# Add and tanh-GELU over 1024 x 4096: other block widths, and a first store that waits for a load

## The chip, the core and the metric

The kernel runs on one core of a Trainium2 chip. The time is device microseconds of one execution; lower is better. The engines that matter here are VectorE (DVE in the profile), ScalarE (ACT), GpSimd (POOL) and SyncE (SP), which issues every DMA of this kernel. The transfers themselves are carried by the core's 16 DMA engines.

## The reference

Two fp32 arrays are added, and the tanh form of GELU is taken of the sum:

```python
def reference(x, y):          # both 1024 x 4096, float32
    z = x + y
    return 0.5 * z * (1 + np.tanh(np.sqrt(2 / np.pi) * (z + 0.044715 * z ** 3)))
```

Each input and the output have 16.78 MB (16384 KB), so 33.55 MB are read and 16.78 MB are written, whatever the tiling.

## The kernel before, in words

The operation is elementwise, so the kernel may cut the arrays as it likes. It sees each array as 128 partitions with `TOT` = 32768 elements in each, and cuts this into three blocks (`blocks`, line 88). A block is one contiguous piece of the DRAM array, laid out as 128 rows, one row for each partition. The rows have 61.25 KB (15680 elements), 64 KB (16384) and 2.75 KB (704). The narrow block comes first in the numbering of columns (0 to 704) and last in DRAM; `rows` (line 90) finds the place. One DMA moves one block of one array, so there are nine transfers: three of x, three of y, three of the output. Each has 128 packets, one for each row.

All of x stays in SBUF in the tile `zt` (named z in the profile); sums and results overwrite it in place. y's narrow block has a tile of its own, `ys`; y's two wide blocks share one tile `yt` (y in the profile) of half the width. So y's second wide block can only be loaded when all adds of the first half that read `yt` are done (`needs[load_y]`, line 188).

SP issues the nine transfers in a fixed order (lines 180 and 181):

```python
sp = [(load_y, 0), (load_y, 1), (load_x, 1), (load_x, 2), (load_y, 2), (load_x, 0)]
sp += [(store, i) for i in (1, 0, 2)]
```

Number 0 is the narrow block, 1 the first wide block, 2 the second. So the order is: y narrow, y first wide, x first wide, x second wide, y second wide (after the adds), x narrow, and then the stores: first wide, narrow, second wide. `begin_early` (line 9) moves the first two of them ahead of the program's opening, and `wait_late` (line 23) moves the wait for the last transfer to the end of the program. Neither is changed.

The compute works on 20 chunks of up to 2048 columns (`chunks`, line 103), numbered by column: chunk 0 is the narrow block, 1 to 8 the first wide block, 9 to 19 the second. A chunk is added by VectorE or GpSimd (`on_vector`, `on_gpsimd`, line 161), and then ScalarE takes the GELU in place (line 173). For some chunks (`copies`, line 104) ScalarE first copies x into PSUM (line 155), and VectorE's add reads it there. GpSimd's first add in the first half is held until VectorE's add of chunk 1 is done (`held`), since it is to run beside adds that read one operand from PSUM. Each engine works through its list in the written order (`on_vector`, `on_gpsimd`, `on_scalar`), under a manual schedule; a store waits for the GELUs of its block (`needs[store]`, line 195).

Of the kernel before, what the change touches and what calls it, by code (L numbers as in the profile page):

```python
# [66 lines left out]
def kernel(  # L67
# [12 lines left out]
    nc = tc.nc  # L80
# [4 lines left out]
    N, D = x.shape  # L85
    assert N % P == 0
    TOT = N // P * D
    blocks = [(704, 16384), (16384, TOT), (0, 704)]

    def rows(array, lo, hi):  # L90
        flat, at = array.rearrange("n d -> (n d)"), 0
        for f, e in blocks:
            if f <= lo and hi <= e:
                own = flat[P * at : P * (at + e - f)].rearrange("(p c) -> p c", p=P)
                return own[:, lo - f : hi - f]
            at += e - f
        raise AssertionError((lo, hi))

    HALF, SLIM = TOT // 2, 704
    xloads = [SLIM, 15680, HALF]  # L100
    yloads = [SLIM, 15680, HALF]
    stores = [SLIM, 15680, HALF]
    chunks = [704, 1344] + [2048] * 7 + [512, 1536] + [2048] * 6 + [1024, 512, 512]
    copies = {2: 0, 3: 2048, 4: 0, 5: 2048, 6: 0, 9: 0, 10: 512, 11: 2048}
    on_vector = [1, 2, 3, 4, 5, 6, 9, 10, 11, 0, 13, 14, 15, 16, 17, 18, 19]
    on_gpsimd = [7, 8, 12]
    on_scalar = [("copy", c) for c in (2, 3, 4, 5, 6)] + [("gelu", 1)] + [("copy", c) for c in (9, 10, 11)] + [("gelu", c) for c in [*range(2, 13), 0, *range(13, 20)]]
    held = {7: 1}

    def ranges(sizes):  # L110
        ends = [sum(sizes[: i + 1]) for i in range(len(sizes))]
# [16 lines left out]
    zt = pool_sb.tile([P, TOT], fp32, tag="z", name="z")  # L128
    yt = pool_y.tile([P, HALF], fp32, tag="y", name="y")
    ys = pool_y.tile([P, SLIM], fp32, tag="ys", name="ys")  # L130
    ps = pool_ps.tile([P, 4096], fp32, tag="ps", name="ps")
    adds = {}

    def in_psum(c):
        a, b = cr[c]
# [6 lines left out]
    def in_y(a, b):  # L142
        return ys[:, a:b] if b <= SLIM else yt[:, a % HALF : a % HALF + b - a]

    def load_y(i):
        a, b = yr[i]
        nc.sync.dma_start(out=in_y(a, b), in_=rows(y, a, b))  # L147

    def store(i):
        a, b = sr[i]  # L150
        nc.sync.dma_start(out=rows(out, a, b), in_=zt[:, a:b])

    def copy(c):
        a, b = cr[c]
# [20 lines left out]
    def earlier_user(c):  # L175
        lo, hi = copies[c], copies[c] + chunks[c]
        before = [k for k in copies if k < c and copies[k] < hi and copies[k] + chunks[k] > lo]
        return [(add, k) for k in before]

    sp = [(load_y, 0), (load_y, 1), (load_x, 1), (load_x, 2), (load_y, 2), (load_x, 0)]  # L180
    sp += [(store, i) for i in (1, 0, 2)]
    pool = [(add, c) for c in on_gpsimd]
    dve = [(add, c) for c in on_vector]
# [5 lines left out]
        copy: lambda c: [(load_x, i) for i in over(xr, *cr[c])] + earlier_user(c),  # L189
        add: lambda c: [(load_x, i) for i in over(xr, *cr[c])]  # L190
        + [(load_y, i) for i in over(yr, *cr[c])]
        + [(copy, k) for k in copies if k == c]
        + [(add, k) for h, k in held.items() if h == c],
# [55 lines left out]
```

## Time and profile before

| | us |
|---|---|
| median of 3 runs | 122.71 (122.63 to 122.83) |
| the profiled execution, its time | 120.94 |
| the profiled execution, its span | 119.5 |
| DVE / ACT / POOL busy in it | 29.2 / 44.1 / 13.8 |

The profiled execution is one run; its span goes from its first to its last instruction or landing, and its time is 1.4 us longer than that. Its rows therefore add up to the span, not to the median of the runs.

In the profile L140 is a load of x, L147 a load of y, L151 a store, L155 a copy to PSUM, L161 an add and L173 a GELU. An engine's name with a q (SPq) is its sequencer: an SPq row is the issue of a DMA, and the DMA lands later. In the view of stretches, DMA packets are counted in the stretch in which they start, with their whole size and time, so the figures of short stretches jump.

### The profile page before, as it was taken

The page shows a single profiled execution, that of the slowest core. Times are in us where ns is not written, and L with a number is a line of the kernel's source. Part 1 is how long each engine was busy: PE and PEld are TensorE (multiplying, and loading weights), DVE is VectorE, ACT ScalarE, POOL GpSimd, SP SyncE. Part 2 cuts the span into 40 slices and gives each one's busy share as a digit, 9 for nine tenths or more (in the row PEclk, how much of TensorE's full clock was granted, in tenths as well). Part 3 has the DMA queues.
Part 4 walks back from the last instruction along what each step waited for, and adds up shares of the span by engine and source line. Part 5 has one row for each costly group of instructions (what it writes and reads, how often), then busy time and mean ns, then how long its engine had stood idle before and what let it go on. Part 6 is the DMA issues. An engine that isn't in the chain of part 4 may idle for free.

```text
span 119.5 us, 118 instructions
## 1 busy us (share of the span) xinstructions
DVE 29.2 (24%) x18; ACT 44.1 (37%) x30; POOL 13.8 (12%) x7
## 2 busy tenths in 40 slices
DVE  0000000000000599970000000029999920000000
ACT  4000000000000588830099999406799980000000
POOL 0000000000000099900000000029200000000000
DMA  9779879977987898889888988997998789998991
GB/s 457 336 336 651 357 336 441 567 336 336 651 357 336 351 702 351 351 351 680 373 351 351 680 373 351 351 457 336 399 567 378 336 362 534 571 395 351 417 571 66
DMA packets 1296, 50.33 MB, mean 421 GB/s; under 512 B 144, under 2 KB 144, under 8 KB 528
## 3 DMA queue, kind: packets, MB, share of 16 engines
q1 hardware_dynamic: 1296, 50.33, 98.6%
HBM read 33.55 MB, written 16.78 MB: 421 GB/s over the span
## 4 chain that ended last, share of the span: by engine, by line
DMA 55%; ACT 13%; DVE 10%; DVEq 3%; issue 0%; ACTq 0%; SPq 0%
DMA z<-in_x_dram 33%; DMA y<-in_y_dram 22%; ACT z L173 11%; DVE z L161 10%; DVEq L216 3%; ACT ps L155 2%; ACTq L216 0%; DVEq L161 0%; SPq L147 0%
## 5 line engine op out<-in xcount | busy, mean ns | idle before, releaser
L173 ACT ACTIVATE z<-z 128x2048 f32<-128x2048 f32 (+5 forms) x20 | 29.7, 1555 | 6.2 <-DVE z L161 6.2
L155 ACT COPY ps<-z 128x2048 f32<-128x2048 f32 (+2 forms) x8 | 13.0, 1654 | 46.4 <-DMA z<-in_x_dram 45.2
L161 DVE TENSOR_TENSOR z<-z,y 128x2048 f32<-128x2048 f32 (+3 forms) x8 | 12.8, 1664 | 38.9 <-DMA z<-in_x_dram 38.9
L161 DVE TENSOR_TENSOR z<-ps,y 128x2048 f32<-128x2048 f32 (+2 forms) x8 | 15.6, 2017 | 27.0 <-DMA y<-in_y_dram 26.7
L161 POOL TENSOR_TENSOR z<-z,y 128x2048 f32<-128x2048 f32 x3 | 13.6, 4533 | 70.4 <-DVE z L161 41.4
L201 ACT ACT_TABLE_LOAD x1 | 1.3, 1283 | 1.3 <-PEq L233 1.3
L161 DVE TENSOR_TENSOR z<-z,ys 128x704 f32<-128x704 f32 x1 | 0.9, 882 | 0.0
L200 DVE MEMSET one<- 128x1 f32 x1 | 0.1, 59 | 1.3 <-PEq L233 1.3
L201 ACT ACTIVATE one<-one 128x1 f32<-128x1 f32 x1 | 0.2, 203 | 0.0
L233 POOL MEMSET const-float32-0.0<- 128x1 f32 x1 | 0.1, 98 | 0.2 <-issue 0.2
L233 POOL MEMSET const-bfloat16-1.0<- 128x1 bf16 x1 | 0.1, 102 | 0.0
L233 POOL MEMSET const-uint8-127<- 128x1 uint8 x1 | 0.1, 102 | 0.0
L233 POOL MEMSET const-float32-1.0<- 128x1 f32 x1 | 0.1, 98 | 0.0
## 6 DMA issues: line engine op xcount, KB each, us to landing
y<-in_y_dram SPq DMA_DIRECT2D x1, 7840.0 KB, 21.2
z<-in_x_dram SPq DMA_DIRECT2D x1, 7840.0 KB, 38.9
out_dram<-z SPq DMA_DIRECT2D x1, 7840.0 KB, 23.1
ys<-in_y_dram SPq DMA_DIRECT2D x1, 352.0 KB, 2.9
z<-in_x_dram SPq DMA_DIRECT2D x1, 352.0 KB, 27.1
out_dram<-z SPq DMA_DIRECT2D x1, 352.0 KB, 11.2
z<-in_x_dram SPq DMA_DIRECT2D x1, 58.0
y<-in_y_dram SPq DMA_DIRECT2D x1, 26.5
```

The lines of the kernel that those rows point to most:

```text
L155: nc.scalar.copy(out=in_psum(c), in_=zt[:, a:b])
L161: ins = eng.tensor_add(out=zt[:, a:b], in0=first, in1=in_y(a, b))
L173: nc.scalar.activation(out=zt[:, a:b], in_=zt[:, a:b], func=act.Gelu_apprx_tanh)
L200: nc.vector.memset(one[:, :1], 0.0)
L201: nc.scalar.activation(out=one[:, :1], in_=one[:, :1], func=act.Gelu_apprx_tanh)
L216: tc.compile()
L233: nc = _bacc.Bacc("TRN2", target_bir_lowering=False, num_devices=1)
```

## The change

The narrow block grows from 704 to 2048 columns (8 KB rows), and the first wide block shrinks from 15680 to 14336 (56 KB rows); the second wide block stays at 16384 (64 KB rows). The lists follow: there are 19 chunks instead of 20, and chunk 0 now has 2048 columns like the seven of the first wide block. The second half's chunks are the same with numbers lower by one. In the first half VectorE adds chunks 1 to 5 and GpSimd 6 and 7, where it was 1 to 6 and 7 and 8, and ScalarE copies four chunks instead of five. After the second wide load of y, VectorE adds the narrow chunk in sixth place of its eleven instead of fourth, and its GELU stands behind those of two more wide chunks.

The first store (number 1) gets a second condition: beside the GELUs of its block it waits until y's second wide load has landed. The wait stands on SP, between the issue of x's narrow load and that of the first store.

```diff
-    blocks = [(704, 16384), (16384, TOT), (0, 704)]
+    blocks = [(2048, 16384), (16384, TOT), (0, 2048)]
...
-    HALF, SLIM = TOT // 2, 704
-    xloads = [SLIM, 15680, HALF]
-    yloads = [SLIM, 15680, HALF]
-    stores = [SLIM, 15680, HALF]
-    chunks = [704, 1344] + [2048] * 7 + [512, 1536] + [2048] * 6 + [1024, 512, 512]
-    copies = {2: 0, 3: 2048, 4: 0, 5: 2048, 6: 0, 9: 0, 10: 512, 11: 2048}
-    on_vector = [1, 2, 3, 4, 5, 6, 9, 10, 11, 0, 13, 14, 15, 16, 17, 18, 19]
-    on_gpsimd = [7, 8, 12]
-    on_scalar = [("copy", c) for c in (2, 3, 4, 5, 6)] + [("gelu", 1)] + [("copy", c) for c in (9, 10, 11)] + [("gelu", c) for c in [*range(2, 13), 0, *range(13, 20)]]
-    held = {7: 1}
+    HALF, SLIM = TOT // 2, 2048
+    xloads = [SLIM, HALF - SLIM, HALF]
+    yloads = [SLIM, HALF - SLIM, HALF]
+    stores = [SLIM, HALF - SLIM, HALF]
+    chunks = [2048] * 8 + [512, 1536] + [2048] * 6 + [1024, 512, 512]
+    copies = {2: 0, 3: 2048, 4: 0, 5: 2048, 8: 0, 9: 512, 10: 2048}
+    on_vector = [1, 2, 3, 4, 5, 8, 9, 10, 12, 13, 0, 14, 15, 16, 17, 18]
+    on_gpsimd = [6, 7, 11]
+    on_scalar = [("copy", c) for c in (2, 3, 4, 5)] + [("gelu", 1)] + [("copy", c) for c in (8, 9, 10)] + [("gelu", c) for c in [*range(2, 14), 0, *range(14, 19)]]
+    held = {6: 1}
...
     def load_y(i):
         a, b = yr[i]
-        nc.sync.dma_start(out=in_y(a, b), in_=rows(y, a, b))
+        yl[i] = nc.sync.dma_start(out=in_y(a, b), in_=rows(y, a, b)).ins
 
     def store(i):
         a, b = sr[i]
-        nc.sync.dma_start(out=rows(out, a, b), in_=zt[:, a:b])
+        ins = nc.sync.dma_start(out=rows(out, a, b), in_=zt[:, a:b]).ins
+        if i == 1:
+            tc.add_manual_dep(
+                ins,
+                yl[2].name,
+                mybir.DependencyInfo(mybir.DependencyClass.Sync, mybir.DependencyReason.DATA),
+                reason="the first store is issued beside the last, narrow load",
+            )
```

More of the change, by code (lines that the diff above doesn't have):

```diff
@@ L131 @@
     ps = pool_ps.tile([P, 4096], fp32, tag="ps", name="ps")
-    adds = {}
+    adds, yl = {}, {}
     def in_psum(c):
```

## The prediction

> **What bounds the kernel now.** I read the head of the page first, then its DMA queue.
>
> ```profile
> span 119.5 us, 118 instructions
> DVE 29.2 (24%) x18; ACT 44.1 (37%) x30; POOL 13.8 (12%) x7
> q1 hardware_dynamic: 1296, 50.33, 98.6%
> ```
>
> No compute engine is busy for half of the span, and the one DMA queue is busy for 98.6% of it. All nine transfers go through that queue in the order in which SP issues them, so the question is where this stream is slowed. The third view is the page's list of DMA issues (KB, us from issue to landing; the last three rows are single transfers from the DMA view), with the timeline of SP for the issue times.
>
> ```profile
> y<-in_y_dram SPq DMA_DIRECT2D x1, 7840.0 KB, 21.2
> z<-in_x_dram SPq DMA_DIRECT2D x1, 7840.0 KB, 38.9
> out_dram<-z SPq DMA_DIRECT2D x1, 7840.0 KB, 23.1
> ys<-in_y_dram SPq DMA_DIRECT2D x1, 352.0 KB, 2.9
> z<-in_x_dram SPq DMA_DIRECT2D x1, 352.0 KB, 27.1
> out_dram<-z SPq DMA_DIRECT2D x1, 352.0 KB, 11.2
> z<-in_x_dram SPq DMA_DIRECT2D x1, 58.0
> y<-in_y_dram SPq DMA_DIRECT2D x1, 26.5
> out_dram<-z SPq DMA_DIRECT2D x1, 21.4
> ```
>
> ```profile
> 0.43 0.42 SPq L147 DMA_DIRECT2D y<-in_y_dram  x1
> 1.26 0.89 SPq L140 DMA_DIRECT2D z<-in_x_dram  x2
> 53.23 0.33 SPq L147 DMA_DIRECT2D y<-in_y_dram  x1
> 53.61 0.43 SPq L140 DMA_DIRECT2D z<-in_x_dram  x1
> 76.13 0.35 SPq L151 DMA_DIRECT2D out_dram<-z  x1
> 88.87 0.34 SPq L151 DMA_DIRECT2D out_dram<-z  x1
> 98.05 0.33 SPq L151 DMA_DIRECT2D out_dram<-z  x1
> ```
>
> Issue plus time to landing gives the landings: y's narrow load 2.9, y's first wide load 21.6, x's first wide load 40.1 (1.26 + 38.9), x's second 59.7 (second of its pair, about 1.7 + 58.0), y's second wide load 79.7, x's narrow load 80.7, first store 99.2, narrow store 100.1, last store 119.4. Differences are the stages: 18.5 us for x's 7840 KB (424 KB a us), 19.6 for x's 8192 KB, **20.0 for y's 8192 KB**, 1.0 for x's 352 KB, 18.5 for the store of 7840 KB, 0.9 for the narrow store, 19.3 for the last 8192 KB. One stage stands out, and it is the one before the first store.
>
> The view of stretches shows it packet by packet. It counts the packets that start in a stretch, and in each of these four stretches one packet starts on each of the 16 DMA engines: 1.00 us at 1049 GB/s is 16 packets of 64 KB, at 1004 GB/s 16 of 61.25 KB. The DMA share is then their mean time in us.
>
> ```profile
> 37.00:38.00 1.00, 0.00 (x0) 0.00 (x0) 0.00 (x0) 1.00 2.32 1004
> 56.00:57.00 1.00, 0.00 (x0) 0.00 (x0) 0.00 (x0) 1.00 2.42 1049
> 75.50:76.50 1.00, 0.00 (x0) 0.61 (x1) 0.00 (x0) 1.00 3.16 1049
> 115.70:116.70 1.00, 0.00 (x0) 0.00 (x0) 0.00 (x0) 1.00 2.42 1049
> ```
>
> The last packets of x's first load take 2.32 us, of x's second 2.42, of the last store 2.42; the last packets of y's second load take 3.16. So 0.74 us is lost on every DMA engine just when the first store, issued at 76.13, stands in the queue behind them. That is the **stall** that the change is about.
>
> **The change, part by part.**
>
> *Sizes.* The bytes stay, 3 x (352 + 7840 + 8192) = 3 x (1024 + 7168 + 8192) = 49152 KB, and so does the packet count, one for each of 128 rows of a transfer. Packet time goes with size: 2.42/2.32 = 1.04, and 64/61.25 = 1.04. So the wide packets lose what the narrow ones gain: 0. The narrow transfers took 1.0 and 0.9 us against 352/424 = 0.83: some 0.1 each is cost by packet, which stays with the count; if longer rows saved it, it would be -0.3 for the three. Rows of 56 KB are in no row of the trace; 61.25 and 64 KB give the same rate within 1%, of which I take 0 and keep +0.2 as the bad end.
>
> *First half.* x's first wide load lands 672 KB earlier, 672/424 = 1.6 us, at 38.5. Its compute then has 14336 columns instead of 15680.
>
> ```profile
> 40.24 1.56 DVE L161 TENSOR_TENSOR z<-z,y 128x1344 f32<-128x1344 f32 x1 [38.85 <-DMA z<-in_x_dram]
> 42.07 11.08 DVE L161 TENSOR_TENSOR z<-ps,y 128x2048 f32<-128x2048 f32 x5 [0.27 <-ACT ps L155]
> 41.88 9.03 POOL L161 TENSOR_TENSOR z<-z,y 128x2048 f32<-128x2048 f32 x2 [41.44 <-DVE z L161]
> 59.71 3.76 ACT L155 COPY ps<-z 128x512 f32<-128x512 f32 x3 [7.80 <-DMA z<-in_x_dram]
> 63.41 12.70 ACT L173 ACTIVATE z<-z 128x2048 f32<-128x2048 f32 x7
> ```
>
> The first add grows from 1344 to 2048 columns (1.56 x 2048/1344 = 2.4, +0.8), and one of five adds and its copy go (11.08/5 = 2.2). y's second wide load, which SP holds until the last of these adds (42.07 + 11.08 = 53.15 before), is issued at 53.2 - 1.6 + 0.8 - 2.2 = 50.2, still 8 us ahead of the landing of x's second load (59.7 - 1.6 = 58.1) that covers it. GpSimd's two adds start 0.8 later after the landing and end near 50 as well. Price 0; cover 8 us. ACT copies (3.7 us from 58.1), then runs six GELUs instead of seven (6 x 1.81 = 10.9) and is done near 72.8.
>
> *The wait.* The first store could thus be issued near 73, and now stands on SP until y's second load lands. Without the stall that is 79.7 - 1.6 - 0.7 = 77.4, a wait of 4.6 us. Behind it on SP are only the narrow store and the last store, due 11 and 20 us later; no engine waits for the store. What it can cost is an empty DMA queue. Its cover is x's narrow load, now 1024 KB, 1024/424 = 2.4 us. The price of an issue on an idle queue: y's narrow load lands 2.9 us after its issue, of which 0.9 is transfer, so 2.0 us of latency at the most; the lower bound is the first packet of the run.
>
> ```profile
> 0.00:1.00 1.00, 0.00 (x0) 0.00 (x0) 0.20 (x4) 1.00 0.00 0
> 1.00:2.60 1.60, 0.06 (x1) 1.33 (x2) 0.00 (x0) 1.00 2.26 853
> ```
>
> Nothing starts before 1.0, so the store's packets are there 1.0 to 2.0 us after its issue, inside the 2.4. An engine that finished y's load some tenths early runs out by at most those tenths: 0, bad end +0.3.
>
> *What the wait is worth.* Before, the store was at the engines from about 77.1 (76.13 + 1.0), with loads left for 80.7 - 77.1 = 3.6 us, 0.8 of it the stall itself (0.74, and 0.06 by which x's narrow load was slower than the narrow store): 2.8 us of work. Now it arrives 1.1 us after y's landing, with 2.4 - 1.1 = 1.3 us of narrow load left. If only a wide load can be stalled, the gain is 0.8; if the stall goes with the load that is left, 0.8 x 1.3/2.8 = 0.4 stays and 0.4 is gained; if it merely moves to the narrow load, 0. I take 0.5, near the middle one, since the store does still lie beside a load.
>
> The Trainium skill, DMA: Bandwidth & Descriptors, section "Two DMAs through the same engine are not ordered", says that descriptors of a queue start in order but are pipelined, with the reading and the writing side apart. By that the reading side turns to the store while loads are still on their way, as the trace bears out: the stall falls on load packets. It also lets the stall move with the store, and then the sum would be 0 instead of -0.5.
>
> *Compute after the landing.* These rows run from y's landing (79.7) to the last store's issue (98.05), 18.3 us.
>
> ```profile
> 79.86 4.55 DVE L161 TENSOR_TENSOR z<-ps,y 128x512 f32<-128x512 f32 x3 [26.71 <-DMA y<-in_y_dram]
> 79.88 4.53 POOL L161 TENSOR_TENSOR z<-z,y 128x2048 f32<-128x2048 f32 x1 [28.96 <-DMA y<-in_y_dram]
> 84.33 0.88 DVE L161 TENSOR_TENSOR z<-z,ys 128x704 f32<-128x704 f32 x1
> 84.45 13.57 ACT L173 ACTIVATE z<-z 128x2048 f32<-128x2048 f32 x10 [0.71 <-DVE z L161]
> 85.13 11.23 DVE L161 TENSOR_TENSOR z<-z,y 128x2048 f32<-128x2048 f32 x7
> ```
>
> The narrow chunk grows from 704 to 2048 columns. On ACT, back to back, that is 1.81 instead of 1.81 x 704/2048 = 0.6, so +1.2; DVE's add grows by 2.2 - 0.9 = 1.3, and DVE ends 96.4 against ACT's 98.0, so ACT stays last, with perhaps 0.1 of waiting. The last store is issued 18.3 + 1.2 + 0.1 = 19.6 after the landing. The queue ahead of it, counted from the same landing, is 2.4 + 7168/424 = 16.9 + 2.5 = 21.8 us. With the 2.0 of latency the last store is ready at 21.6. So the compute hides, as it does now (18.3 + 2.0 = 20.3 against 1.0 + 18.5 + 0.9 = 20.4), by 0.2 us only: this cover is thin, and each tenth that compute loses beyond it is lost at the end.
>
> *Sum.* 0 + 0 + 0 - 0.5 = -0.5 us on a profiled span of 119.5 (run 120.9), so a span near 119.0. The profiled run is 1.8 below the median of 122.71; I carry the difference over: **122.2**.
>
> **The rivals.**
>
> *The stall moves* to x's narrow load, price 0: 122.7, between 122.45 and 122.95. For it: a store is still in the queue beside a load. Against it: x's own narrow packets lost 0.06 where y's wide ones lost 0.74.
>
> *The fetch is paid in the open* (slower). If the engine must be rid of its last load before it can begin on the store, a store that was issued early paid 0.74 for that turn, and one that comes late pays the whole latency after the narrow load: 2.4 + 1.0 to 2.0 = 3.4 to 4.4 us from landing to the store's flow, against 2.4 + 0.8 = 3.2 if the stall had stayed. So it costs +0.2 to +1.2; taken at +0.6, 123.3. It decides where the store flows more than 3.2 us after the landing. Against it: the stall lay on the load's packets, so the fetch began under them. The Trainium skill, same page, section "Rules for kernel authors", says to issue a DMA early so that its fixed cost overlaps other work, which speaks against this wait; the trace here has the cover of 2.4 us over the 2.0 of its first load, and no run yet shows them together.
>
> *Compute becomes the end.* Past the cover of 0.2: were the ten GELUs and adds after the landing 0.1 longer each, the last store would be 0.8 late and eat the gain: +0.3, 123.0. Nothing in the rows makes them longer.
>
> **How the numbers follow.** Stall largely gone: 0.50, its own range 121.85 (0.8, and a little of the narrow rows) to 122.4. Stall moved: 0.22. Fetch in the open: 0.20. Compute: 0.08. Within 0.2% (0.25 us) is about what a measurement cannot tell from no change; so faster 0.50, same 0.22, slower 0.28. The range, 121.8 to 123.1, takes in the first two cases, compute and the lower part of the fetch case, and leaves out some 0.15.
>
> **What would show it.** Right: the last 16 packets of y's second load start near 74 and mean 2.42 us; that load lands near 77.4, and takes 19.4 to 19.6 us after x's; the first store is issued within 0.1 us of it; x's narrow load lands 2.4 to 2.8 us later; last issue near 97.0; the last landing near 118.9. Wrong: narrow packets that take half as long again as the others (the stall moved); no packet starting for some tenths after x's narrow load (the fetch in the open); a gap ahead of the last store's packets (compute).

## The result, and the profile after

The changed kernel takes 120.16 us (median of 6 runs, 120.09 to 120.33). Against the kernel before, run beside it, its time is **0.9928 of it (interval 0.9907 to 0.9949)**, that is 0.7% faster; a second measurement gave 0.9929 (0.9916 to 0.9942). In the batches with the experiments the median of the kernel before was 120.98 to 121.17, so the gain is some 0.9 us. The three runs ahead of the prediction (122.63 to 122.83) are slow ones: over 122 us lie 15 of the 89 runs on record with the old widths and none of the 83 with others, and why is not shown.

The head of the page and its list of DMA issues (KB, us from issue to landing), and SP's issues from the timeline, of the kernel after:

```profile
span 118.8 us, 115 instructions
q1 hardware_dynamic: 1296, 50.33, 98.2%
out_dram<-z SPq DMA_DIRECT2D x1, 7168.0 KB, 19.3
ys<-in_y_dram SPq DMA_DIRECT2D x1, 1024.0 KB, 4.9
z<-in_x_dram SPq DMA_DIRECT2D x1, 1024.0 KB, 29.2
z<-in_x_dram SPq DMA_DIRECT2D x1, 56.7
y<-in_y_dram SPq DMA_DIRECT2D x1, 27.2
out_dram<-z SPq DMA_DIRECT2D x1, 21.5
```

```profile
50.45 0.33 SPq L147 DMA_DIRECT2D y<-in_y_dram  x1
50.83 0.44 SPq L140 DMA_DIRECT2D z<-in_x_dram  x1
77.72 0.35 SPq L151 DMA_DIRECT2D out_dram<-z  x1
97.28 0.33 SPq L151 DMA_DIRECT2D out_dram<-z  x1
```

y's second wide load lands at 50.45 + 27.2 = 77.6, and the first store is issued 0.1 us behind it, where before it was issued 3.6 us ahead of that landing. x's narrow load lands at 50.83 + 29.2 = 80.0, 2.4 us after y's: the pace of 1024 KB without any loss. The stretches show the packets themselves (packets that start in the stretch; DMA share times length is the time that they took on each of 16 engines, GB/s times length their bytes):

```profile
73.90:75.30 1.40, 0.00 (x0) 0.00 (x0) 0.00 (x0) 1.00 1.73 749
77.30:78.30 1.00, 0.53 (x1) 0.00 (x0) 0.52 (x1) 1.00 1.04 442
```

The first row has the 16 last packets of y's second load (1.40 us x 749 GB/s is 16 x 64 KB), at 1.40 x 1.73 = 2.42 us each, where before it was 3.16. The second has 54 narrow packets of x (442 KB in that us, 8.2 KB each) at 1.04 x 16 / 54 = 0.31 us, which is their size at the pace of all others. So the stall of 0.74 us is gone and has not moved. y's second load took 19.3 us after x's (77.6 - 58.3), 0.7 less than before.

### The profile page after: what moved, and what is told of

Its sections match the earlier page's. It is cut to its first block, busy times and chain, and to the rows that moved or that the text cites. A ratio compares the mean times of both kernels' runs of the same rounds, so it can differ in the third digit from the quotient of the medians.

```text
span 118.8 us, 115 instructions
## 1 busy us (share of the span) xinstructions
DVE 29.0 (24%) x17; ACT 42.2 (36%) x28; POOL 13.8 (12%) x7
## 3 DMA queue, kind: packets, MB, share of 16 engines
q1 hardware_dynamic: 1296, 50.33, 98.2%
## 4 chain that ended last, share of the span: by engine, by line
DMA 55%; DVE 11%; POOL 8%; DVEq 4%; ACT 3%; issue 0%; ACTq 0%
DMA z<-in_x_dram 32%; DMA y<-in_y_dram 23%; DVE z L168 11%; POOL z L168 8%; DVEq L223 3%; ACT z L180 3%; ACTq L223 0%; DVEq L168 0%
## 5 line engine op out<-in xcount | busy, mean ns | idle before, releaser
L180 ACT ACTIVATE z<-z 128x2048 f32<-128x2048 f32 (+3 forms) x19 | 29.7, 1628 | 7.3 <-DVE z L168 7.2
L162 ACT COPY ps<-z 128x2048 f32<-128x2048 f32 (+2 forms) x7 | 11.2, 1623 | 46.4 <-DMA z<-in_x_dram 45.1
L168 DVE TENSOR_TENSOR z<-z,y 128x2048 f32<-128x2048 f32 (+2 forms) x8 | 13.6, 1752 | 37.6 <-DMA z<-in_x_dram 37.6
L168 DVE TENSOR_TENSOR z<-ps,y 128x2048 f32<-128x2048 f32 (+2 forms) x7 | 13.4, 1978 | 27.7 <-DMA y<-in_y_dram 27.7
L168 DVE TENSOR_TENSOR z<-z,ys 128x2048 f32<-128x2048 f32 x1 | 2.3, 2284 | 0.0
## 6 DMA issues: line engine op xcount, KB each, us to landing
out_dram<-z SPq DMA_DIRECT2D x1, 7168.0 KB, 19.3
z<-in_x_dram SPq DMA_DIRECT2D x1, 1024.0 KB, 29.2
z<-in_x_dram SPq DMA_DIRECT2D x1, 56.7
y<-in_y_dram SPq DMA_DIRECT2D x1, 27.2
```

The costliest lines, as they stand in the source:

```text
L162: nc.scalar.copy(out=in_psum(c), in_=zt[:, a:b])
L168: ins = eng.tensor_add(out=zt[:, a:b], in0=first, in1=in_y(a, b))
L180: nc.scalar.activation(out=zt[:, a:b], in_=zt[:, a:b], func=act.Gelu_apprx_tanh)
```

## The experiments

Theory A is the prediction's: a store that stands in the queue behind loads slows the last of them. Theory B: it was the narrow load with its rows of 2.75 KB behind y's wide one. Then came the questions of how late the store must be, and what the wait may cost. All ratios are to the kernel before.

**The sizes alone.** The changed kernel without the wait.

```diff
-        if i == 1:
+        if i == 99:
```

> The block widths of the change (56, 64, 8 KB), but the first store has no wait for y's landing, so it is issued when its GELUs are done, near 72.8 us. Theory A (the stall comes from the store standing in the queue behind loads): the last packets of y's second wide load again take about 3.1 us instead of 2.42, or x's narrow packets take over 0.309 us, and the time is within 0.2 us of before (ratio 0.998 to 1.003). Theory B (the stall came from the narrow load with rows of 2.75 KB behind the wide one): all packets at 2.42 and 0.309, the time is that of the changed kernel (ratio 0.993).

Measured: 121.31 us, ratio 1.0017 (0.9993 to 1.0041). Three stretches, the issue of the first store and of x's narrow load, in this run:

```profile
74.20:75.20 1.00, 0.00 (x0) 0.00 (x0) 0.00 (x0) 1.00 2.42 1049
76.60:77.20 0.60, 0.00 (x0) 0.00 (x0) 0.00 (x0) 1.00 0.95 396
78.20:79.20 1.00, 1.00 (x2) 0.63 (x1) 1.00 (x1) 1.00 0.96 205
72.77 0.35 SPq L151 DMA_DIRECT2D out_dram<-z  x1
z<-in_x_dram SPq DMA_DIRECT2D x1, 1024.0 KB, 30.3
```

The last packets of y are clean at 2.42 us, and the stall lies on x's narrow packets: in the third row 25 of them (205 KB) took 0.96 x 16 / 25 = 0.61 us each, **twice** the 0.31 that they take otherwise. Engines are as busy as ever and move half the load data. Each engine's first two narrow packets were at 0.309 us, the next ones at up to 0.72, the last one often at 0.309 again; on average an engine lost 1.0 us. Theory A stands, Theory B falls, and the new sizes by themselves are worth nothing.

The second row shows that the store does not slow the loads as soon as it is in the queue: 29 narrow packets (396 GB/s x 0.60 us is 238 KB) start in it and take 0.95 x 0.60 x 16 / 29 = 0.31 us, 4 us after the store's issue. In the packets of the trace the first slow one starts on each engine 1.2 to 1.8 us before that engine would have been through with its loads at the usual pace.

**The wait alone.** The kernel before with the wait added (the diff's last part, at the old widths).

> The block widths of before (61.25, 64, 2.75 KB), but the first store waits for y's second wide load. Theory A: the last packets of that load take 2.42 us; x's narrow load covers only 0.9 us of the 1.1 to 2.1 us until the store's packets are there, so the DMA engines stand empty for 0 to 1 us after it; gain 0.8 less 0.2 to 0.8 of gap, ratio 0.994 to 1.000. Theory B: the stall of 0.7 us stays on y's last packets and the gap comes on top, ratio 1.002 to 1.008.

Measured: 120.63 us, ratio 0.9959 (0.9929 to 0.9989).

```profile
75.50:76.50 1.00, 0.00 (x0) 0.52 (x1) 0.00 (x0) 1.00 2.42 1049
79.39:79.77 0.38, 0.38 (x2) 0.06 (x1) 0.38 (x1) 1.00 0.00 0
78.93 0.35 SPq L151 DMA_DIRECT2D out_dram<-z  x1
```

No stall on y's packets. But the narrow load of 352 KB is through at 79.39, and the store's first packet starts only at 79.78, 0.85 us after its issue: 0.4 us in which no engine has a packet, more on those that were done sooner. Nearly half of the gain goes back there. The wider narrow block is the cover for the wait, and for that alone it is there.

**The cover by itself.** The changed kernel, the store waiting for x's narrow load, with nothing behind it.

```diff
-                yl[2].name,
+                xl[0].name,      # x's narrow load; xl is kept in load_x
```

> The changed kernel, but the first store waits for the landing of x's narrow load instead of y's wide one, so that nothing covers its issue. It measures the cover by itself: the DMA engines should stand empty from the end of x's narrow packets to the store's first packet, 1.3 to 1.6 us by the latency of 1.0 from the first issue of a run plus the lag of a landing; time 1.2 to 1.6 us over the changed kernel, ratio to before 1.003 to 1.008. If the fetch were prepared in some other way, the gap would be under 0.5 us.

Measured: 121.45 us, ratio 1.001 (0.9976 to 1.0045); its profiled span of 120.0 us is 1.2 over the changed kernel's 118.8.

```profile
79.90 0.35 SPq L151 DMA_DIRECT2D out_dram<-z  x1
79.55:80.74 1.19, 1.19 (x2) 0.80 (x1) 1.19 (x1) 1.00 0.00 0
80.74:81.00 0.26, 0.26 (x1) 0.26 (x1) 0.26 (x1) 1.00 8.26 3529
```

No packet starts between 79.55 and 80.74, and then all 16 engines begin within 0.26 us (3529 GB/s x 0.26 us is 918 KB, which is 16 of the store's packets of 57 KB). So the latency from a store's issue to its packets is 0.84 us, and an uncovered wait costs 1.2 us: the other 0.36 pass from the last packet (79.54) to the issue (79.90), 0.3 of it until the load counts as landed.

**How late is late enough.** In two kernels the store waits for a few copies on ScalarE behind the last GELU of its block instead of y's landing, so that it is issued 0.5 or 1.6 us before that landing.

```diff
+        if c == 7:
+            for _ in range(4):      # 3 in the second kernel
+                delay.append(nc.scalar.copy(out=one, in_=zt[:, 2048:3040]).ins)
...
-                yl[2].name,
+                delay[-1].name,
```

> The changed kernel, but instead of waiting for y's landing (77.6) the first store waits for four copies of 992 columns on ScalarE behind its last GELU, near 76.9 us; the copies write a scratch tile and change nothing else. The run without the wait showed x's narrow packets slowed from the third to the seventh of eight, so a DMA engine turns to the store about 1.9 us before it has written its last load packet. If it is this reading ahead, the store now arrives with 1.1 to 2.0 us of narrow load left, some packets are slowed, x's narrow load loses 0.1 to 0.5 us on each engine, and the time is 0.1 to 0.4 us over the changed kernel (ratio to before 0.994 to 0.997). If only the order of landing and issue mattered, the stall is back in full, 1.0 us (ratio 1.001).

> The same with three copies, so the store is issued near 75.9 and is at the engines with 2.1 to 3.0 us of narrow load left, more than the 1.9 us of reading ahead. Then the stall is there in full, 0.9 to 1.0 us for each engine on x's narrow packets, none of it on y's; ratio 0.999 to 1.003, as without any wait. If the stall goes with the load that is left, it is half of that, ratio 0.997.

Measured: 120.38 us, ratio 0.996 (0.9939 to 0.998), with four copies; 120.98 us, ratio 0.9992 (0.997 to 1.0013), with three. The store's issue and x's narrow load, first with four copies, then with three:

```profile
76.87 0.35 SPq L151 DMA_DIRECT2D out_dram<-z  x1
z<-in_x_dram SPq DMA_DIRECT2D x1, 1024.0 KB, 29.5
```

```profile
75.80 0.35 SPq L151 DMA_DIRECT2D out_dram<-z  x1
z<-in_x_dram SPq DMA_DIRECT2D x1, 1024.0 KB, 30.2
74.00:75.00 1.00, 0.00 (x0) 0.97 (x2) 0.00 (x0) 1.00 2.42 1049
```

In all four kernels with these widths y's load lands 27.2 us after its issue and x's narrow one is issued 0.4 us later, so the time after y's landing gives what the narrow load lost:

| store issued, against y's landing | x's narrow load: issue to landing, us | after y's landing, us | ratio to before |
|---|---|---|---|
| 0.1 us after (the changed kernel) | 29.2 | 2.4 | 0.9928 |
| 0.5 us before (four copies) | 29.5 | 2.7 | 0.996 |
| 1.6 us before (three copies) | 30.2 | 3.4 | 0.9992 |
| 4.6 us before (no wait) | 30.3 | 3.5 | 1.0017 |

The stall grows from 0 to nearly its full size of about 1 us within 1.7 us of issue time, and 3 us more add almost nothing. Counted from the store's arrival at the engines (issue + 0.85, an estimate by the latency measured above) to the landing at the usual pace, the narrow load has 1.5 us left in the changed kernel and pays nothing, 2.1 us with four copies and pays 0.3, 3.2 us with three and pays 0.9 to 1.0. So the stall does not go on growing with the load that is left; there is a reach beyond which a store costs the load the whole of it. The run without the wait puts this reach at 1.2 to 1.8 us before an engine's last load packet ends, which is 1.5 to 2.1 us before the landing, and the table agrees.

**Less cover.** The changed kernel with a narrow block of 1280 columns; chunks, copies and lists follow as in the kernel before.

```diff
-    blocks = [(2048, 16384), (16384, TOT), (0, 2048)]
+    blocks = [(1280, 16384), (16384, TOT), (0, 1280)]
```

> The changed kernel with a narrow block of 1280 columns (5 KB rows) instead of 2048, the wait kept. x's narrow load covers 1.5 us, more than the 0.9 to 1.1 us in which the store's packets come after its issue, counted for the engine that lands last, but not for those that land 0.5 us and more before it. These stand empty for some tenths, and the engines come closer together (landings of the last store 0.3 to 0.6 us apart instead of 0.95). The end is that of the late engines and stays: ratio 0.992 to 0.994. If every engine needs the cover of 2.4 us, the end is 0.3 to 0.6 us later (0.996).

Measured: 119.98 us, ratio 0.9921 (0.9892 to 0.9949), the lowest of all. It was run again beside the changed kernel:

> The changed kernel as it is, run beside the next one for a direct comparison: ratio to before 0.993, about 120.2 us.

> The version with a narrow block of 1280 columns and the wait, on the same chip as the changed kernel. If the shorter narrow load lets the engines come together behind the wait at no cost to the last one, its landings are 0.2 to 0.4 us apart at the end and it is 0 to 0.2 us faster than the changed kernel (ratio to before 0.991 to 0.993). If the earlier result was chance, both are alike within 0.05 us.

Measured: 120.09 us (ratio 0.9929) for the changed kernel and 120.19 us (ratio 0.9934, 0.9921 to 0.9947) for 1280 columns. So the two do not differ; 1.5 us of cover does as well as 2.4. In both profiles of the kernel with 1280 columns the wait brings the engines closer, as was expected: their landings lie 0.53 and 0.59 us apart at x's narrow load and 0.26 and 0.21 at the first store, because the early engines stand empty for some tenths and the last one does not. That saves nothing, since the last engine sets the end. The landings of the last store tell little by themselves: they lie 117.84 to 118.79 in the changed kernel's first profile and 118.20 to 118.53 in its second, a spread that each of these two runs has from its first load on (0.81 and 0.27 us).

**More compute after the landing.** One more copy on ScalarE; it writes a scratch tile. By the edit it stands ahead of the last GELU (chunk 18 of 0 to 18), not of the one before it, as the expectation has it.

```diff
+        if c == 18:
+            nc.scalar.copy(out=one, in_=zt[:, 2048:3040])
```

> The changed kernel with one more copy of 992 columns, about 0.95 us, on ScalarE ahead of the GELU before the last, so that the last store is issued near 98.2 instead of 97.3. By the prediction the cover of the last store is 0.2 us; then the DMA engines stand empty before the last store's packets and the end is 0.6 to 0.8 us later (ratio 0.998 to 1.000). If the latency is 0.9 us as other runs show, the store is at the engines from 99.1, with the first of them done at 98.1 and the last at 99.1: up to 1.0 us of gap on the early engines, none on the last, and the end stays within 0.2 us (ratio 0.993 to 0.995).

Measured: 120.16 us, ratio 0.9934 (0.9912 to 0.9957), no change against the kernel after.

```profile
97.86 0.33 SPq L151 DMA_DIRECT2D out_dram<-z  x1
98.70:98.90 0.20, 0.00 (x0) 0.00 (x0) 0.00 (x0) 1.00 10.73 4588
```

The last store is issued at 97.86, 20.6 us after y's landing of 77.3 instead of 19.6, and 14 engines start on it together at 98.7 to 98.9 (4588 GB/s x 0.20 us is 14 packets of 64 KB), 0.84 us later: they were free by then, and the issue is what they waited for. The end does not move, so 0.9 us more of compute was still covered; that the engines by now wait for the issue suggests that there is no more to be had, which no run tried.

**Wide rows first.** To see whether the short rows at the start cost time, y's first wide load was issued ahead of y's narrow one.

```diff
-    sp = [(load_y, 0), (load_y, 1), (load_x, 1),
+    sp = [(load_y, 1), (load_y, 0), (load_x, 1),
```

> The changed kernel, with y's first wide load issued first and y's narrow load second. The landings of the 16 DMA engines lie 0.8 us apart after the first load in the changed kernel (0.36 in the kernel before) and are as far apart at the end (118.0 to 118.8). If the spread comes from the short rows at the start, wide rows first bring it under 0.5 us and the end is 0.2 to 0.4 us earlier (ratio 0.990). If it comes from the start itself, nothing changes (ratio 0.993).

Measured: 120.28 us, ratio 0.9934 (0.9912 to 0.9956), no difference. The landings of the last store were 0.5 us apart (118.17 to 118.67), but the end did not come earlier. The landings of the first load, now the wide one, were 0.6 us apart (18.89 to 19.48), so the short rows are not what sets the engines apart.

## Why the prediction was right or wrong

*What bounds the kernel* and *the stall*: right. The one queue stays busy for 98.2% of the span, the 0.74 us on y's last packets came from the store behind them, and the change removes it.

*The sum's last line*: wrong, and it alone puts the forecast outside its own range. **The step that failed is "The profiled run is 1.8 below the median of 122.71; I carry the difference over".** The changed kernel does not show that difference: its 12 runs took 120.04 to 120.33, and the median of 120.16 lies beside its profiled run of 120.33. The kernel before does not show it in other batches either (median 120.98 to 121.17, against its profiled 120.94). Counted from the profiled run of before, 120.94 - 0.5 = 120.4 would have been the forecast.

*What the wait is worth*: the mechanism was right and **this term of the sum was mis-sized, by the step "if the stall goes with the load that is left, 0.8 x 1.3/2.8 = 0.4 stays"**, near which 0.5 of 0.8 us was taken as the gain. The whole of it is gained: y's last packets at 2.42 us and x's narrow ones at 0.31. The stall is not shared out over the load that remains; a store that arrives with 1.5 us of load left costs it nothing. On the profiled spans the gain is 119.5 - 118.8 = 0.7, and by the medians some 0.9 us against the 0.5 forecast. The prediction's branch with a gain of 0.8 has the right size for a wrong reason ("only a wide load can be stalled"): in the run of the sizes alone a narrow load lost 1.0.

*Sizes* at price 0: right; alone they gave 1.0017. *First half* at price 0: right (y's load issued at 50.45, forecast 50.2; x's second load at 1.6 + 56.7 = 58.3, forecast 58.1).

*The cover of the wait*: right in its verdict, and too careful in its price. The latency of an issue is 0.84 us, not 1.0 to 2.0: both bounds came from the first load of the run, whose first packet started 1.0 us after its issue. The Trainium skill, DMA: Bandwidth & Descriptors, section "Latency and other measured facts", gives about 0.6 us to the first byte for a DMA issued from SP; the runs here show 0.84 to 0.87 to the first packet. What the narrow load has to cover is a little more, the 1.2 us from the last packet of the awaited load to the store's first: 0.9 us of narrow load left a gap of 0.4, 1.5 us left none on the last engine.

*Compute after the landing*: its times were right (last issue forecast 19.6 us after the landing, measured 97.28 - 77.64 = 19.6), its cover of 0.2 us was wrong by the same latency: 0.9 us more still fitted. The narrow store was put at 11 us behind the first one and came 13.8 behind it (issued at 91.49), since its GELU stands behind two more; nothing waits for it.

*The rival "the stall moves"* is what happens without the wait, or with a store issued 1.6 us before y's landing; at 0.5 us before it about a third is still paid, and the wait escapes it. *The fetch in the open* did not come: no packet of x was late and no gap stood before the store. The Trainium skill, same page, section "Rules for kernel authors", advises to issue a DMA early so that its fixed cost overlaps compute. Here the runs say otherwise for a store behind loads: issued 4.6 us before y's landing it costs 1 us, issued 0.1 us after it costs nothing. Issued too late, with nothing to cover it, it costs 1.2.

*Why* the load runs at half pace while a store stands behind it was not seen directly. The doubled packet times, from the third narrow packet to the last but one, and their start 1.2 to 1.8 us ahead of the end although the store had long been in the queue, fit an engine that reads ahead into the store's data and shares its reading between the two until it can hold no more. The trace records packets as a whole, with no reading side of its own, so that stays an inference.

## What to carry to other kernels

Where one queue carries loads and then stores, and the queue is the bound, look at the time of the last load packets before the first store: if they are longer than their fellows, the store is issued too early. The queue's busy share does not show it: it was 98.2% here with the stall and without it. Issue the store so that it reaches the engines shortly before the last load is through (0.6 and 1.5 us before the landing cost nothing here, 2.1 us cost 0.3), by a wait for the load before the last, and let the last load run longer than the 1.2 us that the wait leaves open. And measure a baseline more than once before its absolute time is carried into a forecast.

## What the runs showed of the hardware

- A store that reaches the queue with 3 us or more of loads ahead slows the last of these to half pace (0.61 us instead of 0.31 for 8 KB packets), for a loss of 0.8 us on each DMA engine on average when it is issued 1.6 us before the landing, and of 1.0 us at 4.6 us before it. A load behind a load does not do this: the last packets of x's two wide loads, with loads behind them, took 2.32 and 2.42 us in the kernel before, like the packets of the last store.
- From the issue on SP to the first packet of a store it took 0.84 to 0.87 us, in the five runs in which some engine was empty by then.
- A wait that empties the engines brings them together: after the uncovered wait, and after the wait alone at the old widths, all 16 started on the store within 0.2 us, and its landings were 0.15 and 0.17 us apart, where those of the load before it had been 0.41 and 0.49 apart. An engine that is ahead can stand empty for some tenths without a cost, which fits that 1.5 us of cover served as well as 2.4.
